# A fused encoder layer on one core: where the gate's splits stand, who moves the last norm factor, where silu's table is loaded, and the zeros of the start

## The chip, the cores and the metric

The kernel runs on one core of one Trainium2 chip. The metric is the device time of one execution in microseconds, the median of several runs. The engines of a core are named as the profile names them: PE (TensorE, products; PEld loads its weights), DVE (VectorE), ACT (ScalarE), POOL (GpSimd) and SP (SyncE, which here only issues transfers).

## The reference

One encoder layer over 1024 tokens of width 1024, in f32: a projection, eight heads of bidirectional retention and eight query heads of windowed attention side by side, an output projection, a norm, a gated feed-forward block with a second gated input `p`, and a norm. Cut to what matters here:

```python
u = x @ W_in
rq, rk, rv, rg, aq, ak, av = split(u)
y = retention_forward(rq, rk, rv) + retention_backward(rq, rk, rv)
y = (y - mean(y)) * rsqrt(var(y) + 1e-5) * gn_gain * silu(rg)   # per head of 64 columns
mix = concat(y, windowed_attention(aq, ak, av, sink)) @ W_out
h = LN1(alpha * x + mix)
f = (silu(h @ W_gate) * (h @ W_up)) @ W_down + sigmoid(h @ W_pg) * (p @ W_pe)
out = LN2(alpha * h + f)
```

## The kernel before

**Products.** Each f32 operand is split into a rounded high part (written by ACT, line 71 or, for weights prepared ahead, 602) and a low part (the rest, written by DVE, line 72 or 603). One f32 product of 128 rows and 512 columns is then three products on PE: high by high, high by low, low by high (lines 77 to 79, and 803 to 805 in the later stages). Line 142 is a row of products of zeros at the very start, before any input is there; nothing reads them.

**Stages.** First the input projections that the first pair of heads needs. Then, for pairs of heads i = 0 to 3, retention and attention. Their own products are small, and between them the projections for the next pair are worked off a queue. A *tick* is one step of that queue. Then come the output projection (line 825 and what it calls, with Strassen-like sums of blocks, from about 354 us), LN1, the gate of `p` with its sigmoid (line 1097), the feed-forward block's gate and up projections in units (from about 539 us, silu at line 1388), the down projection, and LN2.

**What sets the order.** PE's order is written out by hand throughout, and SP's from the output projection on. Until then a scheduler places what stands on the other engines, by the order in which the code hands it over. From LN1 on DVE, ACT and POOL are by hand too, and in the last block all five. Between the ticks, work beside the main line is handed over from a list `later` of pairs (tick, function): at each tick all that is due is called.

**The gate's splits.** `presplit_gate` (line 645) prepares the weight `W_pg` for the products of the later gate. The weight comes in four quarters k, loaded by `load(k)` into the buffers `pre` (one set for k = 1, one shared by 0, 2 and 3). Each quarter gives seven pieces: up to one sum of blocks on DVE (line 663), then `put`, which rounds on ACT into `pro` (602), subtracts on DVE (603), and stores both by SP (604) into memory. The 28 pieces, the load of the last quarter and one empty place make 30 entries; the list `at` gives each its tick, counted from where the list begins, 80 ticks into the main queue. Retention of pair 0 spans ticks 80 to 128, that of pair 1 ticks 128 to 176.

**Retention's own work on the other engines.** `pt` and `qq` (line 411, DVE) are operands of PE's products at line 428. `ptr` (574, ACT) copies the transposed attention weights out of a PE bank, which PE's next transposes (572) write again. `y` (490, DVE) copies a result out of its bank.

**The norm factor.** `norm` (line 494) computes each half pair's factor 1/sqrt(var + eps). It goes in five steps, 3 ticks apart: `spread` lays the two rows of variances out over 128 partitions by a transfer, `power` raises them to −1/2 on POOL (508), `store` writes them to memory (511, SP), `fetch` reads them back, broadcast over 64 partitions, in two transfers (515, SP) into `kv1` or `rb`, and `scaled` multiplies on DVE (519). The last factor is that of pair 3, second half: its `scaled` stands at the start of the output projection. There line 814 loads that projection's operands `w` and `u` by SP, lines 870 to 876 make sums of blocks on DVE, 71 and 72 split them, and ACT's line 972 copies finished products out of the banks.

**Tables.** ACT loads the table of a function when the function is not in the table that it holds; the profile shows this as ACT_TABLE_LOAD. Line 1854 is an activation of one column whose result nobody reads.

Of the kernel before, what the change touches and what calls it, by code (L numbers as in the profile page):

```python
# [11 lines left out]
AF = mybir.ActivationFunctionType  # L12
# [4 lines left out]
P = 128  # L17
# [4 lines left out]
HF = 512  # L22
NPAIR = 4
# [2 lines left out]
ALPHA = 2.0 ** 0.25  # L26
EPS = 1e-5
NKT = 3 * P
WARM = 8
NSC = 4  # L30
LAG = 3
LAGS = (3, 6, 9, 12, 15)
# [10 lines left out]
def layer(tc, xT, xn, w_first, w_mt, w_rv, w_out, w_pg, w_pe, pT, w_gu, w_dn,  # L43
          consts, dec_b, dec_c, sink, gng, lnp, out):
    nc = tc.nc
    act, dve, pool, pe, sp = nc.scalar, nc.vector, nc.gpsimd, nc.tensor, nc.sync
# [12 lines left out]
    def nm(s):  # L59
        uid[0] += 1  # L60
        return f"{s}{uid[0]}"

    def bank(tag, shape=(P, HF)):
        tag = ROLE[tag]
        return ps.tile(list(shape), F32, tag=tag, bufs=NB[tag], name=nm("b" + tag))
# [15 lines left out]
    def behind(ins):  # L81

        tc.add_manual_dep(ins.ins, recent[0], mybir.DependencyInfo(
            mybir.DependencyClass.NoSync, mybir.DependencyReason.DATA), reason="order")
        return ins
# [35 lines left out]
    def a_tile(shape, name, tag=None, dt=F32):  # L121

        turnA[0] += tag is None
        return big.tile(list(shape), dt, tag=tag or f"A{turnA[0] % 2}", bufs=4, name=nm(name))
# [8 lines left out]
    def bt(shape, tag, bufs=None, dt=F32):  # L133
        return bpool.tile(list(shape), dt, tag=tag, bufs=bufs, name=nm(tag))

    zero = bt([P, HF], "sq", 1, mybir.dt.bfloat16)
    pool.memset(zero, 0.0)
    zb = bank("o")  # L140
    for _ in range(WARM):
        pe.matmul(zb, zero[:, :P], zero, start=True, stop=True)
    xr4 = bt([P, 4, S], "rv")
    xraw = [xr4[:, k, :] for k in range(4)] + [bt([P, S], t) for t in ("pt", "qq", "av")] + [bt([P, S], "rk", 2)]
    xs = []
# [4 lines left out]
    with tc.manual_schedule(engines={mybir.EngineType.DVE, mybir.EngineType.SP}):  # L150
        for kt in range(KT):
            r = xraw[kt]
# [240 lines left out]
    class Retention:  # L393
# [100 lines left out]
        def norm(self, hh):  # L494

            b = self.o.rearrange("p n c -> p (n c)")
            for k in range(2):
                pe.matmul(b, ones, self.sq[k], start=k == 0, stop=k == 1)
            row = bt([2, HF], "kv0")
            behind(dve.tensor_scalar(row, b[0:2], 1.0 / 64, EPS, ALU.mult, ALU.add))  # L500
            sm, r, home = bt([P, 2, 8], "sn", 1), bt([P, HF], ("kv1", "rb")[hh]), rnd[2 * self.i + hh]

            def spread():
                for h in range(2):
                    sp.dma_start(sm[64 * h:64 * h + 64, 0], row[h:h + 1].rearrange("o (q e) -> o q e", e=8))

            def power():
                behind(pool.tensor_tensor(sm[:, 1], sm[:, 0], cst[:, C_MH:C_MH + 1].to_broadcast([P, 8]), ALU.pow))

            def store():  # L510
                sp.dma_start(home, sm[:, 1])

            def fetch():
                for h in range(2):
                    sp.dma_start(r[64 * h:64 * h + 64], home[64 * h:64 * h + 64].rearrange("q e -> (q e)").partition_broadcast(64))

            def scaled():
                y = self.half(hh)
                behind(dve.scalar_tensor_tensor(y, y, gn[:, self.i:self.i + 1], r, ALU.mult, ALU.mult))

            later.extend((ticks[0] + at, f) for at, f in zip(LAGS, (spread, power, store, fetch, scaled)))
# [123 lines left out]
    def presplit_gate():  # L645

        first, other = ([a_tile([P, 2, HF], "pre", t) for _ in range(2)] for t in ("A1", "A0"))
        ops = [a_tile([P, 2, HF], "pro", "A1", F32R) for _ in range(2)]
        n = [0]

        def load(k):
            for j in range(2):
                sp.dma_start((other if k == 1 else first)[j], w_pg[j, k])

        def steps(k):
            raw = other if k == 1 else first

            (a11, a21), (a12, a22) = ([raw[j][:, i, :] for i in range(2)] for j in range(2))

            def s(p, x, *sums):  # L660
                def f():
                    for a in sums:
                        behind(dve.tensor_tensor(*a))
                    put(x, ops[n[0] % 2], pgd[p - 1, k])
                    n[0] += 1
                return f

            return [s(1, a11), s(4, a22), s(2, a12), s(5, a22, (a22, a21, a22, ALU.add)),
                    s(7, a21, (a21, a11, a21, ALU.subtract)), s(6, a11, (a11, a22, a11, ALU.subtract)),
                    s(3, a12, (a12, a12, a11, ALU.subtract))]  # L670

        load(0)
        load(1)
        k0, k1, k2, k3 = map(steps, range(4))
        k1[0] = pair_of(k1[0], lambda: load(2))
        k3[0:0] = [lambda: load(3), lambda: None]
        at = [2 + 3.4 * k for k in range(12)] + [55 + 2.5 * k for k in range(2)] + [65 + 1.9 * k for k in range(7)] + \
            [78.5 + 2 * k for k in range(9)]
        return [(ticks[0] + t, f) for t, f in zip(at, k0 + k1 + k2 + k3, strict=True)]

    def pair_of(f, g):
        def both():
            f()
            g()
        return both
# [54 lines left out]
    with tc.manual_schedule(engines={mybir.EngineType.PE}):  # L740
# [17 lines left out]
        r = Retention(0, y0, states)  # L758
# [6 lines left out]
        for i in range(1, NPAIR):  # L765
            assert i == 1 or not side, len(side)
            r = Retention(i, ytile(2 * i), states)
# [419 lines left out]
    frights, fsum = {}, []  # L1187
# [305 lines left out]
    for n in range(NP):  # L1493
        for u in plan(n):
            k = len(gunits)
# [302 lines left out]
    def ahead_g(k, upto):  # L1798

        def finish():  # L1800
            while urgent:
                urgent.pop(0)()

        units = [g[3] for g in gunits] + [2.72]
        room = units[k + 1] - gunits[k][4] - debt[0] if k >= 0 else 100.0
        while items and items[0].unit < upto and items[0].slots <= len(oslots) and (items[0].us <= room or items[0].unit <= k + 1):
            room -= items[0].us
            items.pop(0).issue()
            finish()
        finish()  # L1810
        if held and held[0][0].unit <= k + 1:
            release()
        debt[0] = max(-0.6, -room)
# [25 lines left out]
    with tc.manual_schedule(engines={ET.PE, ET.DVE, ET.Activation, ET.Pool, ET.SP}):  # L1839
        for _ in range(4):  # L1840
            oslots.append(wp.tile([P, 2, HF], F32R, tag="w", bufs=4, name=nm("w")))
            oslots.append(ct([P, 2, HF], "u", 4, F32R))
        sums2.extend(a_tile([P, 2, HF], "sums") for _ in range(2))
        fa = big16((P, 4, 2, 2, Q))
        halves4 = [(fa[:, k, 0], fa[:, k, 1]) for k in range(4)]
        halves4.append(tuple(ct([P, 2, Q], "sg", 2, F32R) for _ in range(2)))
        fsum.extend([cst[:, 0:Q], cst[:, Q:2 * Q], *(ct([P, Q], "fs", 2) for _ in range(2))])
        fwide = ct([P, 2, Q], "p", 2)
        fine, more = fine_right(2, halves4[:3]), fine_right(4, halves4[3:])
        fine += more  # L1850
        homes.update((name, a_tile([P, 2, HF], "ev")) for name in ("spare", "s1", "u2", "c11", "u3", "c22"))
        FINE4 = len(plan(0)) + len(plan(1)) - 2
        FINES = (2, 4, 7, 9, 20, 23, 26, FINE4)
        act.activation(fsum[3][:, 0:1], fsum[0][:, 0:1], AF.Silu)
        ahead_g(-1, 4)
        for k in range(NG):
            gunits[k][1]()
            gunits[k][2]()
            if k in FINES:
                at = max([-1] + [i for i, x in enumerate(items) if x.right]) + 1  # L1860
                for x in fine.pop(0):
                    at += 1
                    x.unit, x.right = items[at].unit, True
                    items.insert(at, x)
                    at += 1
            ahead_g(k, k + 1 + min(9, 4 + k))
            while stores and stores[0][0] <= k:
                stores.pop(0)[1]()
            j = k + 1 - NG
            if j == -6:  # L1870
                while items:
                    items.pop(0).issue()
                release()
                arenas_a()
                op_arena(ct([P, 4, 2, HF], "h0a", dt=F32R))
                arena("chain", ct([P, 8, HF], "h0b"), 8)
            if j == -4:
                for _ in range(3):
                    op_arena(big16((P, 4, 2, HF)))
            if j >= -6:  # L1880
                ahead(0, j + 7)
            if j >= -4:
                ahead(1, j + 5)
        arena("b", big.tile([P, 8, HF], F32, tag="H", bufs=4, name=nm("H")), 8)
        arena("chain", ct([P, 8, HF], "h2"), 8)
        op_arena(ct([P, 4, 2, HF], "h3", dt=F32R), 4)
        rings["op"] += [ct([P, 2, HF], "u", 4, F32R) for _ in range(2)]
        for k in range(ND):
            d_step(k)
# [83 lines left out]
```

## Time and profile before

| | us |
|---|---|
| median of 3 runs | 1171.9 |
| lowest, highest | 1169.49, 1171.92 |
| profiled execution | 1172.7 |
| its span | 1170.6 |

| engine | busy us | share of the span |
|---|---|---|
| PE | 1156.5 | 99% |
| DVE | 900.4 | 77% |
| ACT | 580.1 | 50% |
| POOL | 121.0 | 10% |

The granted clock of PE was 0.998 over the span. In the timelines a row has the start in us, the duration, the engine, the line of the program, the operation, its output and inputs, and a count where several like it are drawn together; in brackets stands how long the engine was idle before it and what ended that. Products of PE overlap: a product of 512 columns has a duration of 0.39 us, but the next one starts 0.23 us after it, so a gap is read from two starts. A row that ends in DMA_DIRECT2D with SPq or POOLq is the issue of a transfer; when it lands is another matter. In a row that has a line, an operation, a count and then three durations, these are least, median and longest in ns. In the rows with KB the last number is the median time in us from issue to landing.

### The profile page before, as it was taken

The numbers are of one execution on the slowest core, as the hardware profiler recorded it, in microseconds if no ns is written. First come the engines' busy times: TensorE is split into PE (matmuls) and PEld (weight loads), VectorE is DVE, ScalarE is ACT, GpSimd is POOL, SyncE is SP. The second block draws the span as 40 slices with busy tenths as digits, with TensorE's granted clock in tenths as the row PEclk, the third lists the DMA queues.
The fourth block names the chain that finished last, engine by engine and source line by source line (L and its number), as shares of the span: only waits on it lengthen the run. The fifth ranks groups of instructions, "written<-read, shape, count | busy, mean of one in ns | idle before, by whom it ended". The sixth has DMA issues, their size and how long they took to land.

```text
span 1170.6 us, 17933 instructions
## 1 busy us (share of the span) xinstructions
PE 1156.5 (99%) x6330; PEld 971.5 (83%) x6330; DVE 900.4 (77%) x1746; ACT 580.1 (50%) x1181; POOL 121.0 (10%) x181
## 2 busy tenths in 40 slices
PE   9999999999999999999999999999999999999996
PEld 7888888788887888888888888888888888888885
DVE  4666688777869688947998988888888976773677
ACT  5566348686756256214445434443344445552463
POOL 2001021202010021000000000000000020133232
PEclk9999999999999999999999999999999999999999
DMA  6345665746356955665322222232223289999977
GB/s 252 100 153 207 246 207 193 244 159 223 127 190 230 365 172 196 261 195 201 117 90 105 112 105 100 102 135 101 99 72 136 89 249 349 350 225 203 261 173 216
DMA packets 84378, 213.86 MB, mean 183 GB/s; under 512 B 12225, under 2 KB 17473, under 8 KB 84289
## 3 DMA queue, kind: packets, MB, share of 16 engines
q1 hardware_dynamic: 75648, 195.94, 47.6%
q0 software_dynamic: 8640, 16.78, 8.2%
q8 instruction: 50, 0.82, 0.3%
q14 instruction: 40, 0.32, 0.1%
HBM read 141.32 MB, written 62.16 MB: 174 GB/s over the span
## 4 chain that ended last, share of the span: by engine, by line
PE 86%; DVE 6%; DMA 4%; ACT 2%; issue 1%; POOL 0%; SPq 0%; DVEq 0%; ACTq 0%; POOLq 0%
PE bmm L803 8%; PE bmm L804 8%; PE bmm L805 7%; PE bt L803 6%; PE bt L804 6%; PE bt L805 6%; PE bmm L77 4%; PE bs L803 4%; PE bs L805 4%; PE bs L804 4%; PE bmm L79 4%; PE bmm L78 4%; PE bo L805 3%; PE bo L803 3%; PE bo L804 3%
## 5 line engine op out<-in xcount | busy, mean ns | idle before, releaser
L77 PE MATMUL bmm<-H,w 128*128 128x512 f32 x240 | 97.3, 405 | 0.0
L78 PE MATMUL bmm<-H,w 128*128 128x512 f32 x240 | 93.9, 391 | 0.0
L79 PE MATMUL bmm<-H,w 128*128 128x512 f32 x240 | 93.9, 391 | 0.0
L1388 ACT ACTIVATE ev<-ev 128x512 f32<-128x512 f32 x42 | 26.5, 630 | 104.3 <-DVE ev L1417 92.8
L1562 POOL DMA_DIRECT2D h0b<-in_w_dn x24 | 21.6, 899 | 540.7 <-DVE ev L1368 504.9
L77 PEld LDWEIGHTS bmm<-H,w 128*128 128x128 f32 x240 | 45.1, 188 | 11.1 <-issue 1.4
L79 PEld LDWEIGHTS bmm<-H,w 128*128 128x128 f32 x240 | 45.1, 188 | 10.3
L78 PEld LDWEIGHTS bmm<-H,w 128*128 128x128 f32 x240 | 45.2, 188 | 7.9
L554 ACT ACTIVATE sc<-sc,st 128x385 f32<-128x385 f32 (+1 forms) x64 | 37.2, 585 | 15.6 <-DVE st L552 15.3
L550 DVE CUSTOM_DVE_ANT_0 sc<-cst,bs,skb 128x384 f32<-128x384 f32 (+1 forms) x64 | 35.0, 575 | 8.3 <-PE bs L549 7.8
L1417 DVE TENSOR_TENSOR ev<-ev,bt 128x512 f32<-128x512 f32 x44 | 30.1, 683 | 12.5 <-PE bt L805 12.5
L1368 DVE TENSOR_TENSOR ev<-ev,bs 128x256 f32<-128x256 f32 x63 | 25.6, 418 | 15.5 <-PE bs L805 14.7
L1390 DVE TENSOR_TENSOR ev<-ev 128x512 f32<-128x512 f32 x42 | 29.0, 691 | 10.5 <-ACT ev L1388 9.0
L803 PE MATMUL bmm<-H,u 128*128 128x512 f32 x92 | 36.2, 393 | 0.2 <-ACT ev L1426 0.2
L804 PE MATMUL bmm<-H,u 128*128 128x512 f32 x92 | 36.0, 392 | 0.0
L805 PE MATMUL bmm<-H,u 128*128 128x512 f32 x92 | 35.8, 389 | 0.0
L72 DVE TENSOR_TENSOR w<-raw,w 128x512 fp32r<-128x512 f32 x34 | 23.1, 688 | 16.2 <-ACT w L71 16.1
L545 POOL COPY sc<-skb 128x1 f32<-128x1 f32 x64 | 15.6, 253 | 188.9 <-PE bt L572 144.5
L560 ACT ACTIVATE sc<-sc,st 128x384 f32<-128x384 f32 (+1 forms) x64 | 34.2, 580 | 1.2 <-DVE st L558 0.9
L71 ACT ACTIVATE H<-ln 128x512 fp32r<-128x512 f32 (+1 forms) x34 | 22.7, 675 | 21.2 <-DVE ln L1052 7.2
L803 PE MATMUL bmm<-H,w 128*128 128x512 f32 x84 | 32.9, 392 | 0.0
L804 PE MATMUL bmm<-H,w 128*128 128x512 f32 x84 | 32.9, 392 | 0.0
(802 smaller groups left out, 3898.4 us busy)
## 6 DMA issues: line engine op xcount, KB each, us to landing
ad<-ev SPq DMA_DIRECT2D x33, 512.0 KB, 2.6
pgd<-pro SPq DMA_DIRECT2D x28, 512.0 KB, 3.0
raw<-in_w_gu SPq DMA_DIRECT2D x22, 512.0 KB, 3.6
ln<-in_w_gu SPq DMA_DIRECT2D x22, 512.0 KB, 3.9
raw<-ad SPq DMA_DIRECT2D x40, 256.0 KB, 5.6
ln<-ad SPq DMA_DIRECT2D x37, 256.0 KB, 6.0
H<-in_w_dn SPq DMA_DIRECT2D x33, 256.0 KB, 7.4
wod<-aq SPq DMA_DIRECT2D x15, 512.0 KB, 2.8
```

The lines of the kernel that those rows point to most:

```text
L77: pe.matmul(o, lh, rh, start=start, stop=False)
L78: pe.matmul(o, lh, rl, start=False, stop=False)
L79: recent[0] = pe.matmul(o, ll, rh, start=False, stop=stop).ins.name
L550: dve.tensor_tensor_reduce(sc[g][:, :nk], cst[:, tc0:tc0 + nk], b[:, :nk], slope(i, g), skb[:, 2 * i + g:2 * i + g + 1], ALU.add, ALU.max, ...
L554: act.activation(sc[g][:, :nk + 1], sc[g][:, :nk + 1], AF.Exp, bias=st_[:, 1, j, g:g + 1], accum_out=st_[:, 2, j, g:g + 1])
L560: behind(act.activation(sc[g][:, :nk], sc[g][:, :nk], AF.Copy, scale=st_[:, 3, j, g:g + 1]))
L803: pe.matmul(o, lh, rh, start=start, stop=False, skip_group_check=True)
L804: pe.matmul(o, lh, rl, start=False, stop=False, skip_group_check=True)
L805: pe.matmul(o, ll, rh, start=False, stop=stop, skip_group_check=True)
L1388: act.activation(c[:, 0, :], c[:, 0, :], AF.Silu)
L1390: dve.tensor_tensor(c[:, 1, :], c[:, 0, :], c[:, 1, :], ALU.mult)
L1417: dve.tensor_tensor(get(name), ev[left][:, m, :], right, ALU.add)
```

## The change

Four edits in one:

- The zeros of the start: the buffer shrinks from 128 x 512 to 128 x 128 and is cleared by DVE instead of POOL; 36 products of 128 columns take the place of 8 of 512.
- `norm`: for the second half of the last pair, `store` and `fetch` go to POOL's queue. All other factors stay on SP.
- `presplit_gate`: other ticks for the same 30 entries. Before, the last stood at tick 94.5 of the list; now it stands at 88.2.
- The one-column silu activation goes from the head of the last block to a place behind the first unit (k = 0) of the feed-forward block.

```diff
-WARM = 8
+WARM = 36
...
-    zero = bt([P, HF], "sq", 1, mybir.dt.bfloat16)
-    pool.memset(zero, 0.0)
+    zero = bt([P, P], "sq", 1, mybir.dt.bfloat16)
+    dve.memset(zero, 0.0)
     zb = bank("o")
     for _ in range(WARM):
-        pe.matmul(zb, zero[:, :P], zero, start=True, stop=True)
+        pe.matmul(zb[:, :P], zero, zero, start=True, stop=True)
...
+            q = pool if hh and self.i == NPAIR - 1 else sp
+
...
             def store():
-                sp.dma_start(home, sm[:, 1])
+                q.dma_start(home, sm[:, 1])
...
             def fetch():
                 for h in range(2):
-                    sp.dma_start(r[64 * h:64 * h + 64], home[64 * h:64 * h + 64].rearrange("q e -> (q e)").partition_broadcast(64))
+                    q.dma_start(r[64 * h:64 * h + 64], home[64 * h:64 * h + 64].rearrange("q e -> (q e)").partition_broadcast(64))
...
-        at = [2 + 3.4 * k for k in range(12)] + [55 + 2.5 * k for k in range(2)] + [65 + 1.9 * k for k in range(7)] + \
-            [78.5 + 2 * k for k in range(9)]
+        at = [2 + 2.8 * k for k in range(14)] + [60 + 1.9 * k for k in range(7)] + [73 + 1.9 * k for k in range(9)]
...
-        act.activation(fsum[3][:, 0:1], fsum[0][:, 0:1], AF.Silu)
         ahead_g(-1, 4)
...
             ahead_g(k, k + 1 + min(9, 4 + k))
+            if k == 0:
+                act.activation(fsum[3][:, 0:1], fsum[0][:, 0:1], AF.Silu)
```

The lines of the changed kernel stand one or two further down than before: 603 is 605, 411 is still 411, 519 is 521, 574 is 576, 972 is 973.

How the change moves instructions is shown at three places. **DVE between pair 1 and pair 2**, around the last copy of pair 1 (`y`, line 490) and the last operands of pair 2's retention (`pt`, 411). A name's first number is its buffer, the second counts through the program. Before, from that copy on, in two pieces:

```order
L490 COPY y228_1596<-bo333_2190 128x512
L491 TENSOR_TENSOR rb337_2222<-qq335_2220,pt336_2221 128x512
L603 TENSOR_TENSOR pro173_1168<-pre169_1164,pro173_1168 128x512
L251 SCALAR_TENSOR_TENSOR aq338_2236<-bmm322_2119,aq338_2236 64x512
L663 TENSOR_TENSOR pre169_1164<-pre168_1163,pre169_1164 128x512
L251 SCALAR_TENSOR_TENSOR aq339_2237<-bmm322_2119,aq339_2237 64x512
L603 TENSOR_TENSOR pro172_1167<-pre169_1164,pro172_1167 128x512
L663 TENSOR_TENSOR pre168_1163<-pre168_1163 128x512
L500 TENSOR_SCALAR kv0345_2280<-bo333_2190 2x512
L663 TENSOR_TENSOR pre168_1163<-pre169_1164,pre168_1163 128x512
L603 TENSOR_TENSOR pro173_1168<-pre168_1163,pro173_1168 128x512
L663 TENSOR_TENSOR pre169_1164<-pre169_1164,pre168_1163 128x512
```

```order
L519 SCALAR_TENSOR_TENSOR y228_1596<-y228_1596,gn_377,kv1318_2110 128x512
L251 SCALAR_TENSOR_TENSOR aq338_2236<-bmm340_2242,aq338_2236 64x512
L411 TENSOR_TENSOR qq357_2330<-bt356_2325,kd_397 128x512
L603 TENSOR_TENSOR pro172_1167<-pre168_1163,pro172_1167 128x512
L251 SCALAR_TENSOR_TENSOR aq339_2237<-bmm340_2242,aq339_2237 64x512
L603 TENSOR_TENSOR pro173_1168<-pre169_1164,pro173_1168 128x512
L72 TENSOR_TENSOR w359_2335<-raw358_2333,w359_2335 128x512
L72 TENSOR_TENSOR w360_2338<-raw358_2333,w360_2338 128x512
L411 TENSOR_TENSOR pt364_2360<-bt363_2355,kd_397 128x512 x2
```

And in the changed kernel, on DVE from the same copy on, the head of the same stretch:

```order
L605 TENSOR_TENSOR pro173_1196<-pre168_1191,pro173_1196 128x512
L665 TENSOR_TENSOR pre168_1191<-pre169_1192,pre168_1191 128x512
L490 COPY y228_1632<-bo333_2229 128x512
L491 TENSOR_TENSOR rb337_2261<-qq335_2259,pt336_2260 128x512
L605 TENSOR_TENSOR pro172_1195<-pre168_1191,pro172_1195 128x512
L251 SCALAR_TENSOR_TENSOR aq338_2276<-bmm322_2153,aq338_2276 64x512
L665 TENSOR_TENSOR pre169_1192<-pre169_1192,pre168_1191 128x512
L251 SCALAR_TENSOR_TENSOR aq339_2277<-bmm322_2153,aq339_2277 64x512
L605 TENSOR_TENSOR pro173_1196<-pre169_1192,pro173_1196 128x512
L500 TENSOR_SCALAR kv0345_2316<-bo333_2229 2x512
L72 TENSOR_TENSOR w359_2363<-raw358_2361,w359_2363 128x512
```

Between the copy and `pt` (line 411) nine pieces of the gate's splits stood (five of line 603, four of 663); three stand there now (605, 665, 605), and the others stand ahead of the copy.

**ACT some 10 us earlier, in pair 1**, around the copies `ptr309` and `ptr311` of attention weights (line 574, in the changed kernel 576). Before:

```order
L587 ACTIVATE y229_1597<-bo277_1878 128x512
L377 ACTIVATE qd306_2074<-cst_367,lq_400 128x128 x2
L71 ACTIVATE w321_2116<-raw319_2111 128x512
L574 ACTIVATE ptr309_2082<-bt308_2078 128x384
L602 ACTIVATE pro172_1167<-pre169_1164 128x512
L240 ACTIVATE rq1305_2069<-bmm288_1944 64x512
L574 ACTIVATE ptr311_2088<-bt310_2084 128x384
```

And in the changed kernel:

```order
L604 ACTIVATE pro173_1196<-pre168_1191 128x512
L377 ACTIVATE qd306_2108<-cst_395,lq_428 128x128 x2
L71 ACTIVATE w321_2150<-raw319_2145 128x512
L604 ACTIVATE pro172_1195<-pre169_1192 128x512
L240 ACTIVATE rq1305_2103<-bmm288_1984 64x512
L576 ACTIVATE ptr309_2116<-bt308_2112 128x384
L576 ACTIVATE ptr311_2122<-bt310_2118 128x384
```

The copy `ptr309` stood ahead of the rounding into `pro172` and now stands behind it; two pieces of the gate's splits (line 604 here) stand in this stretch. They are the first two of the last quarter, which is loaded shortly before; the piece of line 602 in the rows of before still belongs to the quarter before it.

**SP and ACT at the head of the output projection.** Before, on SP:

```order
L505 DMA sn598_3719<-kv0597_3717 64x1x8 x2
L511 DMA rnd_451<-sn598_3719 128x8
L604 DMA ped_453<-aq481_3046 128x1024
L515 DMA rb599_3720<-rnd_451 64x512 x2
L814 DMA u612_3835<-wod_455 128x1024
L814 DMA w613_3837<-wod_455 128x1024
```

And in the changed kernel, on SP:

```order
L507 DMA sn598_3747<-kv0597_3745 64x1x8 x2
L606 DMA ped_481<-aq481_3074 128x1024
L815 DMA u612_3863<-wod_483 128x1024
L815 DMA w613_3865<-wod_483 128x1024
L815 DMA u614_3867<-wod_483 128x1024
```

The store (511) and the fetch (515) have left SP's order; on POOL they stand right behind the power of line 508 (510 in the changed kernel). On ACT, in the stretch in which the output projection's first results are copied out (`h0b`, line 972), before:

```order
L1854 ACT_TABLE_LOAD
L1854 ACTIVATE fs842_5352<-cst_367 128x1
L71 ACTIVATE H622_3852<-ln623_3853 128x512 x2
L71 ACTIVATE H621_3851<-ln624_3854 128x512
L972 ACTIVATE h0b640_3990<-bt636_3938 128x512
L71 ACTIVATE H622_3852<-ln624_3854 128x512
```

And in the changed kernel:

```order
L71 ACTIVATE h3627_3925<-y354_2351 128x512
L71 ACTIVATE H622_3880<-ln623_3881 128x512 x2
L71 ACTIVATE H622_3880<-ln624_3882 128x512
L973 ACTIVATE h0b640_4018<-bt636_3966 128x512
L71 ACTIVATE H621_3879<-ln624_3882 128x512
```

The load of silu's table is gone from here, and the first copy `h0b` stands behind the splitting of `H622`, which stood behind it.

## The prediction

> **What bounds the kernel now.** I read first the page's share of each engine, then the waits of PE, then the timelines around the places that the edits touch.
>
> ```profile
> span 1170.6 us, 17933 instructions
> PE 1156.5 (99%) x6330; PEld 971.5 (83%) x6330; DVE 900.4 (77%) x1746; ACT 580.1 (50%) x1181; POOL 121.0 (10%) x181
> ```
> TensorE (PE) is busy 99% of the span. Only a few microseconds of gaps are there to be won, and any gap that an edit opens in PE is added to the time in full. The order of PE's products after the first zeros is the same in both kernels, so the change of the time is the change of PE's gaps.
>
> ```profile
> PE bt L428 <- DVE pt L411: 2.0, 1, 2.0
> PE bo L142 <- POOL sq L139: 1.3, 1, 1.3
> ...
> PE bt L803 <- DMA u<-wod: 0.4, 1, 0.4
> ```
> This view lists whom PE waited for: total, times and longest wait. There is one large wait (2.0 us, for VectorE's `pt` of line 411); the start comes next, and the rest is waits of 0.6 us and less, of which the one for `u` and three others come up below. Each edit can be laid against one or two of them. The profiled execution took 1172.7 us, 0.8 above the median of the runs shown (1171.9); I make the sum against it and take 0.8 off at the end.
>
> **Edit A: the zeros.** The rows of the start:
>
> ```profile
> 0.73 0.52 POOL L139 MEMSET sq<- 128x512 bf16 x1 [0.29 <-POOLq L1962]
> 1.31 3.60 PE L142 MATMUL bo<-sq 128*128 128x512 bf16 x8 [1.31 <-POOL sq L139]
> 4.17 0.63 ACT L71 ACTIVATE H<-rv 128x512 fp32r<-128x512 f32 x1 [2.16 <-DMA rv<-in_xT]
> 4.85 0.79 PE L77 MATMUL bmm<-H,w 128*128 128x512 f32 x1
> 5.87 0.41 PE L77 MATMUL bt<-H,w 128*128 128x512 f32 x1
> ```
> GpSimd's memset takes 0.52 us and PE's zeros start at 1.31. They run at 3.60 / 8 = 0.45 us a product, and the real products begin at 4.85, just after the input that ScalarE converts (4.17 + 0.63 = 4.80). That input comes by a transfer, which the edit does not touch, so the first real product can't move forward. VectorE writes a quarter of the columns; its first zero products can start at most some 0.35 us sooner (most of the 0.52). The zeros are now 36 x 128 = 4608 columns against 4096, at the same columns per time 0.45 x 4608 / 512 = 4.05 us, so they end at about 1.31 − 0.35 + 4.05 = 5.0, level with 4.85 within 0.2. No row shows a product of 128 columns at the low rate of the start. If each carries a fixed cost that makes it dearer than a quarter of 0.45, the zeros overrun the real data: 20 ns more each would be 0.7 us, but the first real products run slowly up to 5.87 anyway, so at most about 0.6 of it is lost. The other bound: if PE's rise to its full rate, seen between 4.85 and 5.87, follows the start of the zeros, it comes 0.35 us earlier, which saves half of that, 0.17, and with fewer slow real products up to 0.4. I take **−0.1** (−0.4 to +0.6), nearest to equal columns at the rate of the row.
>
> The Trainium skill, "TensorE: Matmul & The Clock Gate", Part 1, says that the window which lifts the clock is free-running and does not start with the kernel's first product; by that the earlier start buys nothing and A would be 0 instead of −0.1. No run so far shows the rise with another start.
>
> **Edit C: the spread of the gate's splits.** These pieces are two-engine work: ScalarE rounds (line 602), VectorE subtracts (603) or first adds (663).
>
> ```profile
> L603 DVE TENSOR_TENSOR pro<-pre,pro 128x512 fp32r<-128x512 f32 x5 | 3.4, 686 | 0.4 <-ACT pro L602 0.4
> L663 DVE TENSOR_TENSOR pre<-pre,pre 128x512 f32<-128x512 f32 x3 | 2.0, 683 | 0.0
> L663 DVE TENSOR_TENSOR pre<-pre 128x512 f32<-128x512 f32 x1 | 0.7, 683 | 0.0
> ...
> 216.19 0.69 DVE L490 COPY y<-bo 128x512 f32<-128x512 f32 x1 [1.65 <-ACT pt L489]
> 230.73 1.28 DVE L411 TENSOR_TENSOR pt<-bt,kd 128x512 f32<-128x512 f32 x2
> 232.16 1.04 PE L428 MATMUL bt<-rv,pt 128*64 128x64 f32 x28 [1.97 <-DVE pt L411]
> ```
> The first three rows group VectorE's work from 216.1 to 231 us: five pieces of line 603 and four of 663 stand between the copy at 216.19, for which VectorE had been idle 1.65 (its queue was empty there), and `pt` at 230.73, for which PE stands still 1.97 us. In the changed order three of the nine are left behind the copy. The six others leave this stretch: at 0.62 us each (four similar operations take 2.49 us in a row quoted below) that is 3.7 us, more than the 1.97 that PE lacks, with 1.7 to spare. So this wait goes. What is late next at that place is nothing that I can see, as the same queue holds the other operands too.
>
> ```profile
> 164.00:222.00 58.00, 57.72 (x452) 48.43 (x451) 46.68 (x116) 43.00 (x104) 11.62 (x22) 1.00 0.56 191
> ...
> 181.17 0.39 PE L79 MATMUL bmm<-H,w 128*128 128x512 f32 x1
> 181.84 0.88 PE L572 MATMUL bt<-cst,sc 128*128 128x128 f32 x6 [0.28 <-ACT ptr L574]
> 206.72 0.45 SPq L653 DMA_DIRECT2D pre<-in_w_pg  x1
> 213.19 0.63 ACT L602 ACTIVATE pro<-pre 128x512 fp32r<-128x512 f32 x1 [0.98 <-DMA pre<-in_w_pg]
> 205.96 0.49 ACT L574 ACTIVATE ptr<-bt 128x384 f32<-128x384 f32 x1
> 207.04 0.82 PE L572 MATMUL bt<-cst,sc 128*128 128x128 f32 x6
> ```
> The first row is a stretch of 48 ticks, 58 us long, with PE's busy time behind it: a tick is 1.2 us here. From 181.17 to 181.84 PE loses 0.44 beyond the 0.23 that a product takes, for a late `ptr`. Three pieces stood in VectorE's order between the softmax steps ahead of it, and they have moved into the stretch before; I count it as won. The pieces cost something where they now stand. The fourth quarter of the weight is loaded as ever a few ticks before its use: the second of its loads, issued at 206.72, landed at 213.19, 6.5 us later, and ScalarE stood 0.98 for it. Now load and use are 0.3 tick closer (some 0.3 us), and all lies 5.5 ticks earlier. ScalarE's order there becomes: piece, piece that waits for this load, then the evictions `ptr` of line 574, which had come ahead of them. Behind the waiting instruction they are late: 206.72 − 6.6 + 6.5 = 206.6 for the landing, then 0.6 for the piece, 0.6 for another and 0.5 for `ptr` make 208.3, while PE's product at 207.04 needs that bank. It is ready at 206.45 now. That is a new gap of 1.2 us; if the load is issued with the slots free, as its place in the changed order lets it, 0.3 or none. I take 0.5. C is −1.97 − 0.44 + 0.5 = **−1.9** (−2.4 to −1.2).
>
> **Edit B: the last factor's store and fetch on GpSimd.**
>
> ```profile
> 347.05 0.33 SPq L511 DMA_DIRECT2D rnd<-sn  x1
> 348.49 1.11 SPq L515 DMA_DIRECT2D rb<-rnd  x2
> 353.06 0.75 DVE L519 SCALAR_TENSOR_TENSOR y<-y,gn,rb 128x512 f32<-128x512 f32 x1 [1.62 <-DMA rb<-rnd]
> 353.73 2.49 DVE L72 TENSOR_TENSOR H<-y,H 128x512 fp32r<-128x512 f32 x4
> 365.82 0.58 ACT L972 ACTIVATE h0b<-bt 128x512 f32<-128x512 f32 x1
> 372.44 0.58 ACT L972 ACTIVATE h0b<-bs 128x512 f32<-128x512 f32 x1
> 373.07 0.50 PE L803 MATMUL bs<-w,H 128*128 128x512 f32 x1 [0.55 <-ACT h0b L972]
> ...
> L1562 POOL DMA_DIRECT2D h0b<-in_w_dn x24: 863/874/1184, 948.1 to 1124.1; - x24
> rb<-rnd SPq DMA_DIRECT2D x8, 128.0 KB, 3.3
> h0b<-in_w_dn POOLq DMA_DIRECT2D x24, 256.0 KB, 7.0
> h<-in_w_dn POOLq DMA_DIRECT2D x9, 256.0 KB, 5.3
> h0b<-in_w_dn SPq DMA_DIRECT2D x8, 256.0 KB, 5.6
> h<-in_w_dn SPq DMA_DIRECT2D x3, 256.0 KB, 5.1
> ```
> SP stores the factor at 347.05, waits for the landing and fetches it twice at 348.49; SP's own later loads (`u<-wod`, PE's wait of 0.4) stand behind these. With the two steps on GpSimd, SP issues them about 3 us sooner, and that wait goes. But VectorE is the next bound: line 519 starts when the factor lands, 353.06, and from there VectorE works without a gap for over 20 us, ScalarE's evictions of line 972 come in that rhythm, and PE's product at 373.07 waits for one of them. A gap saved earlier is waited out there; the stretch moves with the start of line 519.
>
> The price of that start: a GpSimd issue takes 0.87 us (row of 1562) against 0.55 on SP (1.11 / 2), and transfers of one size land later from GpSimd than from SP, by 5.3 − 5.1 = 0.2 to 7.0 − 5.6 = 1.4 us. Store: on SP 348.49 − 347.05 = 1.4 to landing, so 1.6 to 2.8, landed 348.7 to 349.9. Second fetch: issued 0.9 later, and landing after 3.3 (the median of `rb<-rnd`) to 4.0 (as here: 353.06 − 348.49 − 0.55), plus 0.2 to 1.4. Line 519 then starts between 353.1 and 356.2; the middle of both gives 354.7. One of VectorE's operations of line 72 (0.62) now stands ahead of line 519 and is done by then, so the rest moves by 354.7 − (353.06 + 0.6) = +1.0, and ScalarE's first eviction of line 972 (365.82) now stands behind one more operation of its own, which I put at 0.2. B is **+1.2** (−0.45 to +2.7). Behind the two steps in GpSimd's order stand only the variances of LN1, which need results of this very stretch.
>
> The Trainium skill, "DMA: Bandwidth & Descriptors", Latency and other measured facts, puts the first byte at about 1 us from GpSimd and 0.6 from SP. With 0.4 for each of the two dependent transfers line 519 would start at about 354.2, B would be +0.7, and the sum half a microsecond lower. The pairs of rows above, 0.2 and 1.4, lie on both sides of that figure.
>
> **Edit D: silu's table.**
>
> ```profile
> 362.84 1.28 ACT L1854 ACT_TABLE_LOAD   x1
> 549.79 1.28 ACT L1388 ACT_TABLE_LOAD   x1 [2.41 <-DVE ev L1417]
> 557.50 0.39 PE L805 MATMUL bmm<-H,w 128*128 128x512 f32 x1
> 558.09 0.50 PE L803 MATMUL bmm<-H,u 128*128 128x512 f32 x1 [0.20 <-ACT ev L1426]
> ```
> The load at 362.84 is wasted: sigmoid's table comes between, and silu's is loaded again at 549.79, with ScalarE's chain behind it up to the eviction for which PE waits at 558.09. Now the early activation stands behind the first FFN unit, where ScalarE idles 2.41 us before 549.79; the load is off the chain, 1.28 against a gap of 558.09 − 557.50 − 0.23 = 0.36. At 362.84 ScalarE has 1.28 us less to do, but it waits for VectorE there, so nothing is won. If that idle time did not cover it, an eviction of line 1424 would be 1.3 late; PE has a second bank. D is **−0.3** (−0.5 to 0).
>
> **Sum:** −0.1 − 1.9 + 1.2 − 0.3 = −1.1, so 1171.6 for an execution like the profiled one, and 1170.8 against the median.
>
> **The rivals.** (1) *The factor is no later on GpSimd.* For it: GpSimd is idle, its step follows its own power without another engine between, and the pair 5.3 / 5.1 is near equal. Against it: the dearer issue. Then B −0.45, C −2.4, D −0.5, A −0.3: −3.6, and 1168.3. (2) *ScalarE, crowded by the moved pieces, gives the gain of C back*: the load lands as late as its 6.5 us, the two evictions behind it are late, and VectorE's softmax after them. C is 0, the sum +0.8, the time 1172.7. For it speaks the new order on ScalarE; against it, that PE has other products between. (3) *Slower: GpSimd's transfers take as long as line 1562's slow ones*, whose median is 7.0 us for 256 KB. Store 4 us, issue 0.9, fetch 7: line 519 starts at 359, the stretch is 5.3 late, the sum +3.0, the time 1174.9. It decides, with the other terms as forecast, from a start of line 519 at about 358 on. Against it: this fetch has 128 KB and lands in 4 us from SP.
>
> **How the numbers follow.** My forecast of a small gain has 0.42, rival 1 has 0.28, rival 2 0.13, rival 3 0.17. A difference under 0.2% (2.3 us) can't be told from none. The forecast, 1170.8 with its own range of 1169.0 to 1172.6, lies mostly within it, as rival 2 does; rival 1 lies below. Faster: 0.25 of rival 1 and 0.11 of the forecast, 0.36; slower: rival 3 and a little of rival 2, 0.19; the same: 0.45. The range goes from below rival 1's time, 1167.2, to short of rival 3's, 1174.2.
>
> **What would show it.** A right: zeros start near 1.0 and end near 4.9, first real product at 4.85. C right: no wait of PE for `pt` near 230 us, and a new short wait of PE for `ptr` near 207. B right: line 519 starts between 353 and 357, no wait for `u<-wod`, and a longer wait of PE for line 972. D right: one table load fewer, no wait for line 1426. A start of line 519 beyond 358, or zeros that end after 5.5, would make the forecast wrong upwards; no wait for 972 at all, downwards.

## The result, and the profile after

The changed kernel takes 1184.4 us (1182.96 to 1186.31, 4 runs) against 1170.7 (1168.61 to 1171.92): a ratio of 1.012, with a 95% interval of 1.0095 to 1.0145, some 14 us more. Its profiled execution took 1182.96 us, its span is 1180.8. That is 1.4 below its median, while the profiled execution of the kernel before (1172.7) lies 2.0 above its own, so the two traces are only 10 us apart: places read from them do not carry the whole 14.

PE's waits in the changed kernel, the longest first (total, times, longest):

```profile
PE bt L806 <- DVE H L72: 5.2, 1, 5.2
PE bs L550 <- DVE pt L461: 1.4, 3, 0.7
PE bt L428 <- DVE pt L411: 1.2, 2, 0.9
PE bo L142 <- DVE sq L139: 1.0, 1, 1.0
...
PE bmm L77 <- DVE aq L251: 0.6, 1, 0.6
```

The wait of 2.0 for `pt` near 230 us is gone, as forecast. A new one of 5.2 stands in its place at the head of the output projection, and small ones are spread over retention and attention. PE's order is the same in both kernels, so each product can be set against itself; the difference of its two starts is how far the changed kernel is behind:

| product that starts in the kernel before at | behind by, us |
|---|---|
| 13 | −0.40 |
| 158 | −0.41 |
| 176 | +1.71 |
| 228 | +1.89 |
| 234 | −0.57 |
| 268 | +1.84 |
| 308 | +3.81 |
| 355 | +3.97 |
| 376 | +10.07 |
| 561 | +10.17 |
| the end | +10.00 |

Two places make it: 4 us between 158 and 308, and 6 us between 355 and 376. One execution can differ from the next by 1 to 2 us at such a place without any edit there, as b_store and b_factor show below. The second place, in the timelines of GpSimd, SP, VectorE and PE:

```profile
350.99 0.79 POOL L513 DMA_DIRECT2D rnd<-sn  x1 [0.33 <-POOL sn L510]
357.58 1.06 POOL L517 DMA_DIRECT2D rb<-rnd  x2 [5.79 <-PE bmm L79]
...
349.93 0.33 SPq L606 DMA_DIRECT2D ped<-aq  x1
350.62 0.33 SPq L815 DMA_DIRECT2D u<-wod  x1
351.05 0.45 SPq L815 DMA_DIRECT2D w<-wod  x1
351.55 0.49 SPq L815 DMA_DIRECT2D u<-wod  x1
...
363.69 0.75 DVE L521 SCALAR_TENSOR_TENSOR y<-y,gn,rb 128x512 f32<-128x512 f32 x1 [7.61 <-DMA rb<-rnd]
365.10 0.79 PE L806 MATMUL bt<-u,H 128*128 128x512 f32 x1 [5.20 <-DVE H L72]
...
354.00:376.00 22.00, 16.80 (x66) 13.39 (x65) 14.36 (x24) 9.91 (x18) 1.06 (x2) 0.84 0.47 159
```

GpSimd's store of 4 KB goes out at 350.99, lands after 6.0 us, and the fetch that waits for it goes out at 357.58: 6.6 us from store to fetch, against 1.4 before. (The bracket of its row names PE as what ended the wait, but here and in b_factor, bcd and b_hold the fetch goes out 0.5 to 0.6 us after the store's landing, so it is the landing that it waits for.) The factor is there 6.1 us later, at 363.69, against 4.6. Around the store stand four transfers of 512 KB: a store of SP that was there before too, and three loads that SP no longer holds back. The last row is the stretch from 354 to 376 us: granted clock 0.84 in the third number from the end. After its gap PE runs at the low rate for some 4 us (products 0.43 us apart instead of 0.23), which costs nearly 2 us on top of the 5.2.

In this execution the start gained 0.4 us:

```profile
0.98 3.69 PE L142 MATMUL bo<-sq 128*128 128x128 bf16 x36 [0.98 <-DVE sq L139]
4.90 0.50 PE L77 MATMUL bmm<-H,w 128*128 128x512 f32 x1 [0.23 <-ACT H L71]
5.24 0.39 PE L77 MATMUL bs<-H,w 128*128 128x512 f32 x1
```

The zeros are through at 4.7 and PE has its full rate from the first real product on. That is the luck of this execution. Edit A alone (a_zeros, below) starts its zeros at the same 0.98, and there PE is 0.55 behind the kernel before:

```profile
0.98 4.02 PE L142 MATMUL bo<-sq 128*128 128x128 bf16 x36 [0.98 <-DVE sq L139]
6.71 0.54 PE L78 MATMUL bmm<-H,w 128*128 128x512 f32 x1
7.09 0.40 PE L79 MATMUL bmm<-H,w 128*128 128x512 f32 x1
7.32 0.40 PE L78 MATMUL bs<-H,w 128*128 128x512 f32 x1
```

Its products are 0.43 us apart up to 6.7 and 0.23 apart from 7.1 on. The ten kernels that keep the old zeros all start them at 1.31, and there the full rate begins anywhere from the first real product on (4.8 us, b_factor) to 7.3 us (b_store).

### The profile page after: what moved, and what is told of

The parts are those of the page before. It is cut to its first block, busy times and chain, and to the rows that moved or that the text cites. A ratio compares the mean times of both kernels' runs of the same rounds, so it can differ in the third digit from the quotient of the medians.

```text
span 1180.8 us, 17985 instructions
## 1 busy us (share of the span) xinstructions
PE 1160.3 (98%) x6358; PEld 975.3 (83%) x6358; DVE 902.1 (76%) x1747; ACT 578.3 (49%) x1180; POOL 123.0 (10%) x183
## 4 chain that ended last, share of the span: by engine, by line
PE 84%; DVE 6%; DMA 4%; ACT 3%; issue 1%; POOL 0%; SPq 0%; DVEq 0%; ACTq 0%
PE bmm L804 8%; PE bmm L805 8%; PE bmm L806 8%; PE bt L804 6%; PE bt L805 6%; PE bt L806 6%; PE bs L806 4%; PE bs L805 4%; PE bs L804 4%; PE bo L806 4%; PE bo L805 4%; PE bo L804 4%; PE bmm L77 4%; PE bmm L79 3%; PE bmm L78 3%; DMA pgd<-pro 2%
```

## The experiments

Each time stands beside runs of the kernel before on the same chip (medians of 1170.23 to 1171.03 in the five groups).

| kernel | median us (runs) | ratio to before, 95% interval |
|---|---|---|
| a_zeros | 1172.57 (10) | 1.0015, 1.0005 to 1.0024 |
| b_factor | 1178.79 (4) | 1.0065, 1.0045 to 1.0086 |
| c_spread | 1170.67 (10) | 0.9997, 0.9986 to 1.0007 |
| d_table | 1170.34 (10) | 1.0000, 0.9991 to 1.0010 |
| b_store | 1172.56 (8) | 1.0022, 1.0009 to 1.0035 |
| b_fetch | 1176.70 (3) | 1.0056, 1.0033 to 1.0079 |
| b_hold | 1176.41 (3) | 1.0052, 1.0029 to 1.0075 |
| b_act | 1178.06 (4) | 1.0061, 1.0023 to 1.0099 |
| a_count | 1174.12 (8) | 1.0030, 1.0018 to 1.0043 |
| a_dve8 | 1170.83 (12) | 1.0002, 0.9993 to 1.0012 |
| acd | 1177.12 (6) | 1.0054, 1.0039 to 1.0069 |
| cd | 1170.88 (12) | 1.0003, 0.9995 to 1.0012 |
| w48 | 1173.77 (9) | 1.0024, 1.0014 to 1.0034 |
| bcd | 1177.94 (6) | 1.0063, 1.0051 to 1.0075 |
| w16 | 1173.22 (12) | 1.0018, 1.0008 to 1.0028 |
| w24 | 1174.35 (11) | 1.0023, 1.0015 to 1.0032 |

### One edit at a time

The kernel before with edit A, B, C or D alone, each as in the change's diff.

> Edit A alone. Theory 1 (each part of the change acts by itself, as PE's offsets between the two traces read): PE at its full rate from the first real product on, 0.4 to 0.5 us faster than before, and an offset of PE that stays at -0.4 to the end. Rival (the earlier start of the first stages is given back at a later wait on ScalarE, VectorE or a transfer): no gain, offset back at 0 by the end of the first pair. The difference is under what the runs can tell from none; the trace decides.

> Edit B alone. Theory 1 (the store and the fetch are slow from GpSimd by themselves): store some 6 us to landing, line 519 (521 here) starts 9 to 11 us after GpSimd's power ends instead of 6, the stretch of the output projection costs 5 to 6.5 us, time +5 to +6.5. Rival (they were slow because edit C had made this stretch late against other transfers): store 1.6 to 2.8 us, factor at about 354.7, time +1 to +1.5, as predicted.

> Edit C alone. Theory 1 (C is the loss of 4.4 us that stands between 160 and 345 us in the changed kernel's trace): PE loses about 2 us around 164 to 176, wins 3 at about 230, and loses it again plus 2 more by 310; time +4 to +5. Rival (the predicted gain is there, and what ate it is chance of the transfers in that execution): the wait for pt near 230 is gone and the time is 1 to 3 us lower.

> Edit D alone. Theory 1: no wait of PE for line 1426 at about 558, offset of PE -0.5 from there on, five table loads instead of six; time -0.5. Rival (the load only moves to another place of ScalarE's chain): an eviction of line 1424 is late and PE waits 0.5 to 1.3 before 552; time 0 to +1.

B alone costs 7.6 us (ratio 1.0065), about half of the whole. Its store takes 5.6 us to landing without C, so the rival, that C had made this stretch late, is out. A, which was to gain half a microsecond, costs 1.8 (interval 0.6 to 2.8). C and D do not differ from the kernel before. The four ratios add up to some 9 us, not 14: A and C together do something that neither does alone. So the first theory on C failed (4 to 5 us more), and the gain of 1 to 3 us that the rival gave does not show either (−0.4 us, interval −1.6 to +0.8). The gain near 230 us is there in its trace (behind by −0.31 before that place, −2.78 after it), and 1.5 of it is given back by 268 us, the first part at once:

```profile
229.42 0.99 PE L428 MATMUL bt<-rv,pt 128*64 128x64 f32 x28
230.34 1.16 PE L459 MATMUL bs<-rq,rk 64*128 64x128 f32 x16
...
234.52 0.44 PE L548 MATMUL bs<-k,aq 128*128 128x384 f32 x1 [0.76 <-DVE pt L461]
```

These are PE's products in c_spread: no gap before `pt` of line 411, and 5 us further PE waits for VectorE's next operand, of line 461. The same wait stands in cd and bcd (0.6 each). So part of what PE had lost at 230 is lost again there. In d_table no wait for line 1426 is left, silu's table is loaded at 543.24 and its products near 558 come without the gap: PE moves from −1.98 to −2.47 there, the 0.5 expected, too little for the runs to show.

### What makes the store and the fetch slow

```diff
 b_store:
-                sp.dma_start(home, sm[:, 1])
+                q.dma_start(home, sm[:, 1])
 b_fetch:
-                    sp.dma_start(r[64 * h:64 * h + 64], home[...])
+                    q.dma_start(r[64 * h:64 * h + 64], home[...])
 b_hold (edit B, and in fetch):
+                if q is pool:
+                    sp.dma_start(sm[:, 0], home)
 b_act (edit B with):
+            q = act if hh and self.i == NPAIR - 1 else sp
```

> Of edit B only the store goes to GpSimd; the fetch stays on SP and waits there for the store's landing, so SP's loads for the output projection stay behind the fetch as before. Theory 1 (GpSimd's path is slow by itself): the store still takes 5 to 6 us to landing, line 521 starts 4 to 5 us later than before, time +4 to +5. Theory 2 (in edit B the store is slow because SP's loads, no longer held up, run at the same time): the store lands after 2 to 3 us, line 521 starts 1 to 1.5 us later, time 0 to +1.5.

> Of edit B only the fetch goes to GpSimd; the store stays on SP, ahead of the loads. Theory 2: the store lands after 1.5 to 3 us as it is issued ahead of the loads, and the fetch, issued among them, takes 5 to 6 us: line 521 2 to 4 us later, time +2 to +4. Theory 1: the fetch alone is slow by GpSimd's path, 5 us and more with or without the loads, time about the same; b_hold tells the two apart on the fetch.

> Edit B, and SP reads the stored factor once more into a small tile that nothing uses: with that, SP waits for the store's landing again, and its loads for the output projection go out only then. Theory 1: store 5 to 6 us, time +5 to +7, as with edit B. Theory 2: the store lands after 2 to 3 us, the fetch still runs beside the loads (4 to 5.5 us), time +1 to +3.

> Edit B with ScalarE's queue in place of GpSimd's: the store and the fetch do not stand in SP's order, so SP's loads go out early, but no transfer is issued by GpSimd. Theory 1: store 1.4 to 2.1 us as from SP, factor no later than before, apart from what ScalarE's waiting for the store costs its own evictions. Theory 2: the store takes 4 to 6 us among the loads, as from GpSimd, and the factor is as late as in edit B.

The rows of b_store, with the loads behind SP's fetch:

```profile
348.82 0.78 POOL L513 DMA_DIRECT2D rnd<-sn  x1 [0.33 <-POOL sn L510]
350.79 1.10 SPq L517 DMA_DIRECT2D rb<-rnd  x2
351.94 0.58 SPq L816 DMA_DIRECT2D u<-wod  x1
...
354.78 0.75 DVE L521 SCALAR_TENSOR_TENSOR y<-y,gn,rb 128x512 f32<-128x512 f32 x1 [1.27 <-DMA rb<-rnd]
```

GpSimd's store is through in 2.0 us when no load runs beside it. The kernel still costs 2.6 us (1.1 to 4.1), more than the 0 to 1.5 of theory 2, and its trace does not show that cost here: PE is behind by 2.1 at 340 us and by 1.7 at 376. What its trace does show is a loss of 1.4 us between 228 and 250, as b_factor's does (1.9), where neither differs from the kernel before. Both traces have the low rate there, behind PE's gap of 2.0 us for `pt`; the row is b_store's stretch from 232 to 236 us, with the granted clock 0.57 (0.61 in b_factor, 1.00 in the kernel before):

```profile
232.00:236.00 4.00, 3.68 (x45) 3.43 (x45) 3.19 (x12) 2.43 (x9) 0.00 (x0) 0.57 0.73 243
```

In b_act GpSimd issues nothing:

```profile
346.06 0.42 SPq L816 DMA_DIRECT2D u<-wod  x1
...
346.36 0.35 ACTq L513 DMA_DIRECT2D rnd<-sn  x1
351.15 1.16 ACTq L517 DMA_DIRECT2D rb<-rnd  x2
...
359.56 0.75 DVE L521 SCALAR_TENSOR_TENSOR y<-y,gn,rb 128x512 f32<-128x512 f32 x1 [5.11 <-DMA rb<-rnd]
```

Here the store from ScalarE's queue takes 4.8 us and the fetch 8.4, in the company of the loads that SP issues from 346.06 on. So the loads make the store slow, not GpSimd's path: theory 2. In b_hold the store, ahead of the loads, took 2.0 us (issued at 346.76; SP's own read of it goes out at 348.75), and the fetch, issued at 349.23 together with the loads, lasts until 356.77, 7.5 us. In b_fetch the store from SP is as quick, and the fetch from GpSimd goes out at 348.51, behind the first two loads (347.39 and 347.90), and is there at 357.86, 9.4 us later. b_hold and b_fetch cost more than theory 2 expected (6.1 and 6.6 us against 1 to 3 and 2 to 4): it put the fetch's share too low. A fetch from GpSimd with no load beside it was not run, so a smaller share of GpSimd's path in the fetch is not excluded.

### Why edit A costs

In a_zeros PE is level with the kernel before up to 250 us (behind by 0.2 to 0.55) and falls back to 3.1 by 308. The first rows that differ are ScalarE's, then the landing of the stores `wod<-y`, first of the kernel before, then of a_zeros:

```profile
249.59 0.63 ACT L602 ACTIVATE y<-y 128x512 fp32r<-128x512 f32 x1
DMA to landing us min/median/max: 2.6/2.6/3.4
```

```profile
252.00 0.63 ACT L602 ACTIVATE y<-y 128x512 fp32r<-128x512 f32 x1 [2.18 <-DMA wod<-y]
DMA to landing us min/median/max: 2.6/2.7/4.8
q8 instruction: 1, 0.02, 4.2%
```

The store issued at 247.2 lands after 4.8 us instead of 2.6, and ScalarE, which writes that buffer next, waits. The last row is the view of the transfers from 247.5 to 250 us: the queue of instructions moved one packet of 16 KB there. In the kernel before the view shows none in that stretch, and one from 253.5 to 256. PE's code is fetched in such pieces through the same transfer engines: the queue moves 50 of them in the span, for 12,660 products and weight loads, one for some 250 of them. Edit A puts 56 instructions more at its head (28 products, each with its weight load), so most later pieces are fetched sooner, the one near 250 us by 6.0 us and others by 0 to 7 (up to 340 us). The store of 267.6 meets the next piece (269.3) and lands after 5.4 us instead of 3.8; ScalarE waits 0.96 for it at 273. PE loses 1.1 us at 265 and 1.8 between 290 and 302, waiting for VectorE's operands; the steps from ScalarE to these waits were not followed one by one. Two kernels part A's halves, with two that combine the edits:

```diff
 a_count:
-WARM = 8
+WARM = 36
-    zero = bt([P, HF], "sq", 1, mybir.dt.bfloat16)
+    zero = bt([P, P], "sq", 1, mybir.dt.bfloat16)
-        pe.matmul(zb, zero[:, :P], zero, start=True, stop=True)
+        pe.matmul(zb[:, :P], zero, zero, start=True, stop=True)
 a_dve8:
-    pool.memset(zero, 0.0)
+    dve.memset(zero, 0.0)
 acd: the whole change without edit B
 cd: edits C and D
```

> Of edit A only the number of products: GpSimd clears the 128 x 128 zeros as before, 36 products of 128 columns. Theory 1 (A costs by the 56 more instructions in PE's stream: PE's code, fetched in pieces of 16 KB over the same transfer engines, is fetched 3 to 6 us earlier, and one such piece falls on a store of the weight splits at 247 us for which ScalarE waits): the piece comes at about 248 us, that store lands after 4.5 to 5 us, ScalarE waits some 2 us, time +1.5 to +2.5 as with edit A. Rival (A costs by what VectorE does at the start or by when the zeros begin): time 0 within 1 us, the store after 2.6 to 3.4 us.

> Of edit A only the engine: VectorE clears the 128 x 512 zeros, 8 products of 512 columns as before. Theory 1: PE's code is fetched when it was before (the piece at about 254 us), no late store at 247 us, time 0 or up to 0.4 below. Rival: time +1.5 to +2.5 as with edit A.

> The whole change without edit B. Theory 1 (with C's stores at other times, A's earlier code fetch falls on two of them, at about 151 and 249 us, as in the changed kernel's trace): PE 3 to 4.5 us later than before at 340 us, time +2.5 to +4.5. Rival (A, C and D only add up, +2.2, +0.3 and 0): time +2 to +2.5 with no late store near 150 us.

> Edits C and D alone. Theory 1: no late store, no wait for pt at 230 us, no wait at 558: 0 to 1.5 us below the kernel before. Rival (C gives back later what it wins at 230, whatever the code fetch does): 0 to +1.

It is the number of products. With GpSimd's memset and 36 products the store takes 4.5 us, ScalarE waits 1.8 and the kernel costs 3.5 us, more than the 1.5 to 2.5 expected; with VectorE's memset and 8 products the stores near 250 take up to 3.3, nothing waits for them and it costs nothing (0.2). acd costs 6.3 us where cd costs 0.4: beside C's stores the shifted fetches cost more than alone, more too than the 2.5 to 4.5 expected. Its stores of `wod` at 249 and 269 us take 4.8 and 5.7, and PE loses 0.8 at 164 us, 1.5 at 186 and 2.3 between 290 and 302. cd shows no gain (+0.4 us, −0.6 to +1.4). Its trace has the late `ptr` near 207 us that the prediction had priced at 0.5 (PE falls from −0.55 to −0.02):

```profile
207.03 0.93 PE L572 MATMUL bt<-cst,sc 128*128 128x128 f32 x6 [0.36 <-ACT ptr L574]
```

> The kernel before with 48 products of 86 columns at the start (4128 columns; 80 more instructions in PE's stream than before, 24 more than with edit A). Theory 1 (not the number of instructions costs, but where the code fetches that they shift fall): the piece that comes at 254 us before and at 248.5 with 36 products comes at about 246, in the gap between the stores of 242 and 247 us; no store of wod takes over 3.5 us, no wait of 2 us on ScalarE near 250, time 0 within 1.2 us, unless another piece meets another store. Rival (more instructions in the stream cost by themselves, wherever the pieces fall): time +3 or more.

> The whole change without edit A. Theory 1 (A's shifted code fetch costs 4 to 6 us beside C, B some 7): +7 to +9, that is 5 to 7 below the whole change, with no store of wod over 3.5 us near 250. Rival (A costs in the whole change only the 2 to 4 us that it costs alone): +10 to +12.

```diff
 w48 (w16: 16, 256; w24: 24, 172):
-WARM = 8
+WARM = 48
-        pe.matmul(zb, zero[:, :P], zero, start=True, stop=True)
+        pe.matmul(zb[:, :86], zero[:, :P], zero[:, :86], start=True, stop=True)
 bcd: the whole change without edit A
```

w48 did not tell the two apart: the piece came at 248.0, not in the gap, the store took 4.6 us, and the kernel costs 2.8. bcd answered its question: all but A is 7.4 us, so A takes some 6.5 of the whole change's 14, give or take 3 by the intervals.

> The kernel before with 16 products of 256 columns at the start (4096 columns as before, 16 more instructions in PE's stream). Theory 1 (a code fetch costs where it meets a store that ScalarE waits for): the piece that comes at 254 us before comes at 252 to 253.5, beside the store of 251 us, whose landing ScalarE needs only at 255.5: the store of 247 us lands after 2.6 to 3.4 us, time 0 within 1 us. Rival (instructions cost by themselves, 28 more products cost 2 to 4): +0.6 to +1.2.

> The kernel before with 24 products of 172 columns at the start (4128 columns, 32 more instructions). Theory 1: the piece comes at 250 to 252 us, after the data of the store of 247 us; that store lands after 2.6 to 3.4 us and ScalarE does not wait 2 us near 250: time 0 within 1.2 us. If the piece comes before 249.5 again, the store is late and the time +2 or more. Rival (instructions cost by themselves): +1.2 to +2.2 with the store on time.

Both failed in the total (2.1 and 2.7 us instead of none, which is nearer to the rival's 0.6 to 1.2 and 1.2 to 2.2) and were right near 250: in w16 the piece comes at 253.8, the store of 247 us is on time and ScalarE does not wait; in w24 it waits 0.3. What they lose they lose elsewhere. Rows of w16, from ScalarE, the landing of the stores `pgd<-pro`, and PE:

```profile
156.64 0.63 ACT L602 ACTIVATE pro<-pre 128x512 fp32r<-128x512 f32 x1 [3.55 <-DMA pgd<-pro]
DMA to landing us min/median/max: 2.6/3.0/7.6
165.15 0.47 PE L77 MATMUL bmm<-H,w 128*128 128x512 f32 x1 [0.54 <-DVE aq L251]
q8 instruction: 1, 0.02, 3.7%
```

The last row is the stretch from 150.5 to 152.5 us: another piece of code comes there and meets another store, whose landing grows from the 6.6 of the kernel before to 7.6. ScalarE waits 3.55 instead of 2.50, and PE loses 1 us at 164. w24 and the whole change lose there as well, with their pieces at 150.3 and 151.6; a_zeros, with its piece at 147.9, does not. w24 loses again between 290 and 302 (1.2 us), where its store of 266.6 takes 5.3; w16's store of 267.7 takes 3.6, and it loses nothing there. So 16 instructions can cost at a place where 56 cost nothing. Where a piece falls decides, as far as these traces go. None of these kernels has more instructions and all pieces clear of such stores, so that the number alone costs nothing is not shown.

## Why the prediction was wrong

**A.** The zeros did as worked out: they started 0.33 us sooner and ended at 4.7 (5.0 in a_zeros, as worked out), and the first real product stood at 4.90. The 0.4 that the start gained was luck: a_zeros lost 0.55 there. The term of −0.1 failed by what it left out: the 56 instructions that stand in front of all later code. Their price is 1.8 us alone, and beside C and D 5.9 (acd 1.0054 against cd 1.0003). The sum had no term for it, and no rival named it. On the rise of the rate the rule cited from the Trainium skill, "TensorE: Matmul & The Clock Gate", Part 1, fits better than a rise that follows the zeros: with zeros that start at 0.98, PE is at its full rate at 4.9 us in the changed kernel and only from 7.1 in a_zeros.

**B.** The failing sentence is "With the two steps on GpSimd, SP issues them about 3 us sooner, and that wait goes". The loads did go sooner and the wait did go; but the sum took this for a gain and priced the two transfers by rows in which nothing new runs beside them. The store took 6.0 us where 2.8 was the upper bound, line 519 started at 363.7 where 356.2 was. Rival 3 had the size (it decided from 358 on) and the wrong cause: slow transfers of GpSimd. b_store and b_act show it is the loads. One page that I did not weigh bears on it: the Trainium skill, "DMA: Bandwidth & Descriptors", Issuing engines are not separate DMA queues, has all transfers run on the same 16 engines whoever issues them, and only the issuing time saved. b_act agrees: 4.8 us for a store of 4 KB. The cost was then sized from VectorE's chain alone; the low rate after PE's gap of 5.2 us, nearly 2 us, was missing too.

**C.** The wait for `pt` went, and PE moved by 2.5 us there in c_spread, as the step had it; the 0.44 near 182 was won too (from +0.13 to −0.31). The new gap near 207 that it priced at 0.5, and that was rival 2, did not come in c_spread but came in cd (0.53) and bcd (0.68). What the step missed was given back one step on, at line 461. "What is late next at that place is nothing that I can see" was the wrong step: VectorE's queue behind `pt` was late as well. Alone C is worth −0.4 us (−1.6 to +0.8), not −1.9. How much of that is the stores at new times rather than the order on VectorE was not tried.

**D.** Right in mechanism, and in size at the edge of its range (0.5 at 558 us in d_table, where −0.3 with a bound of −0.5 was forecast); too small for the runs.

## What to carry to other kernels

A small transfer on the critical path can be protected by its queue: here SP's wait for it held back the large loads that stood behind it. Moving it to an idle queue frees those to compete: before such a move, list what the old queue will issue during the transfer's life, and price the transfer among that. And instructions that fill idle time at the start were not free here: they shifted the later fetches of PE's code, so compare the landing times of the transfers that are waited for, over the whole span, before counting the gain.

## What the runs showed of the hardware

- PE's code came in packets of 16 KB over the transfer engines, each taking 0.9 to 2.3 us in the records; near 247 us a store of 512 KB that met one landed after 4.5 to 5.1 us (a_zeros, a_count, acd, w48 and the changed kernel) instead of 2.6 (before, a_dve8, cd, bcd, w16 and w24).
- A gap of 5.2 us in PE was followed by some 4 us at the low rate, with a granted clock of 0.84 over the 22 us around it. A gap of 2.0 us near 230 was followed by it in b_store and b_factor, and not in the kernel before.
- With the same zeros from 1.31 us on, PE's full rate stood from the first real product on in b_factor (4.8 us), and only from 7.3 us on in b_store.
- A store of 4 KB landed after 1.4 us (SP, kernel before) to 1.9 us (GpSimd, b_store) with one store of 512 KB beside it, and after 4.8 (ScalarE's queue, b_act) to 6.0 us (GpSimd's, the changed kernel) with three loads of 512 KB more.
